# A small matmul folded into its neighbour's weights, and six scheduling edits, in a decoder block on eight cores

## The chip, the cores and the metric

One Trainium2 chip, all eight NeuronCores (two dies of four), each core working on two of the sixteen sequences. The metric is device time in microseconds (us) of the slowest core. Most executions agree within 0.3%. In some executions the cores of one die, or of both, run at a lower granted TensorE clock and the time is several per cent longer; these are called slow and are never compared with fast ones.

Every experiment ran beside the kernel before on the same chip, but not all experiments on the same chip. On the chip of the first profiles die 0 lost time to spells at 0.81 of the clock. On the chips of the later experiments these spells were nearly absent from the fast runs, so the kernel before took some 2572 us there instead of 2593.

## The reference

```python
x = x + 0.5 * swiglu(rmsnorm(x, ffn1_norm), ...)          # 1024 -> 2816 -> 1024
h = rmsnorm(x, mix_norm) @ w_in                            # pool values | q | k | v | forget logits
# pooling mixer on 512 columns: 4 groups of 128 channels, windows 2, 4, 8, 16
pooled = causal_window_mean(groups[g], w_g) - groups[g]    # along the tokens
mixed  = einsum("bsgc,gcd->bsgd", pooled, pool_w)          # along the channels
y_pool = rmsnorm(mixed * pool_scale, out_norm_pool)
y_attn = rmsnorm(forgetting_attention(q, k, v, f, ...), out_norm_attn)
x = x + concat([y_pool, y_attn]) @ w_out
x = x + 0.5 * swiglu(rmsnorm(x, ffn2_norm), ...)
```

Sixteen sequences of 2048 tokens, width 1024, 8 attention heads of 64.

## The kernel before

The two FFNs run as eight units of 1024 tokens each; the mixer (projection, pooling, attention, output projection) runs as eight tiles of 512 tokens, interleaved with the FFN units. Nobody wrote the interleaving by hand: each piece is a Python generator that yields operations, and a list scheduler picks, when the program is built, the operation that its estimates say can start first. After that the order on each engine is fixed.

```python
def emit(self, op):                                   # the scheduler's clock, cut
    ...
    done = t + cost + LAT[op.eng]
    late += cost + LAT[op.eng] + LATE                 # LATE = 300.0: pessimism, steers the order
```

Eight PSUM banks come from one pool, `MB`. Attention holds five of them through a tile. "Credits" limit how many results of one kind may be on their way:

```python
def project():                                        # cut
    for t in range(NT):
        cred = Pool_(2)                               # two results in flight: v, q, k, pool alike
        ...
        sc.spawn(pool_post(t, pb, cred), P_POST)
        for it in range(6):                           # q, q, k, k, pool, pool
            for c2 in range(2):
                yield cred
                b = yield MB
                yield Op("pe", ..., mm8(w, c2 * 1024, b, hm), ...)      # L759

def pool_post(t, banks, cred):                        # cut
    if t:
        yield ev_an[t - 1]                            # attention norm of the tile before
    for g in range(4):
        yield Op("act", ..., e.copy(out=pv[:, 16:528], in_=ps[bank][:]))      # L849
        MB.put(bank); cred.put(0)
        ... window sums on VectorE (L866) ...
        yield Op("dve", ..., scalar_tensor_tensor(out=pl, ...))               # L877: mean - input
        mb = yield MB
        yield Op("pe", ..., e.matmul(ps[mb][:], lhsT=poolw[g], rhs=pl))       # L889
        yield Op("act", ..., e.activation(out=slot(g), in_=ps[mb][:], func=Copy,
                                          scale=pool_scale))                  # L893
        MB.put(mb)

def norm_ffn(u):                                      # cut; statistics for each unit's two tiles
    for t2 in range(2):
        yield XS                                      # the one buffer for a tile of the residual
        yield from x_loads(xf, s, tt, ...)            # reload it from memory
        r, rs_ = yield from (stats_pool() if u else stats_pe(x_))   # squares summed on POOL, or on TensorE
```

Of the other lines named below: L710 is the gate/up matmul of an FFN, L736 the down matmul, L637 and L640 the ScalarE copy and the VectorE multiply that free a gate/up pair's banks, L953 and L961 attention's matmuls, L998 the ScalarE step between them, L553 the ones-matmul that sums squares, L1081 the add of the residual behind the output projection. L885 belongs to the same VectorE chain as L877.

## Time and profile before

| | before |
|---|---|
| time, median of the first 4 runs | 2589.9 us |
| TensorE busy, idle (core 1, complete trace) | 2470.4 us, 113.2 us |
| busiest other engine | ScalarE, 59% |
| idle in front of the pool_w matmul, 0.3% of the matmuls | 31.7 us |

TensorE is the bound, so the question to the profile is what its idle time consists of; the prediction below shows these lines.

### The profile page before, as it was taken

Reading aid. Unit: us, or ns where it says so; the run is one execution under the profiler, and the core shown is the slowest. Engines: PE = TensorE matmul, PEld = TensorE weight load, DVE = VectorE, ACT = ScalarE, POOL = GpSimd, SP = SyncE. Lnnn points to the kernel's source line nnn. Section 1 sums busy time; section 2 is a strip of 40 time slices with the busy share of each in tenths; the row PEclk is TensorE's granted clock in tenths of the full one; section 3 lists DMA queues with packets and bytes.
Section 4 is the critical chain, followed back from the end, with each engine's and each line's share of the span. In section 5 each row is a group of like instructions: output and inputs, shape, how many; then the busy total and the mean of one; then the engine's idle time right before and its main releaser. Section 6 shows DMA issues by size and latency. Waiting matters only on the chain.

```text
span 2588.8 us, 39912 instructions; the slowest of 8 cores (2559.3 to 2588.8 us)
## 1 busy us (share of the span) xinstructions
PE 2452.7 (95%) x11667; PEld 1063.9 (41%) x11900; DVE 1388.9 (54%) x1827; ACT 1528.5 (59%) x3137; POOL 1067.4 (41%) x1147
## 2 busy tenths in 40 slices
PE   7999998989998999999999989998999899999999
PEld 2444443434343444334444433443344344444444
DVE  2112147765667775764755847635767566642111
ACT  5562467661766835788455668257784579904650
POOL 2444435541544532545334426444354134514430
PEclk8989999999999999999999999999999999999999
DMA  7888866358635455652555242652525531275225
GB/s 169 175 210 203 225 148 170 98 161 237 174 113 158 122 180 166 174 155 66 178 172 167 103 147 75 190 171 79 180 80 172 194 109 66 66 213 162 74 66 161
DMA packets 123876, 383.56 MB, mean 148 GB/s; under 512 B 15152, under 2 KB 15280, under 8 KB 123056
## 3 DMA queue, kind: packets, MB, share of 16 engines
q0 software_dynamic: 51664, 206.33, 30.7%
q1 hardware_dynamic: 72000, 174.67, 20.3%
q8 instruction: 100, 1.64, 0.3%
q14 instruction: 112, 0.92, 0.1%
HBM read 348.05 MB, written 91.24 MB: 170 GB/s over the span
## 4 chain that ended last, share of the span: by engine, by line
PE 78%; DMA 6%; DVE 5%; issue 5%; ACT 4%; POOL 1%; SPq 0%; DVEq 0%; ACTq 0%; POOLq 0%
PE ps L710 41%; PE ps L736 20%; PE ps L759 9%; PE ps L961 2%; PE ps L953 2%; PE ps L1141 2%; DMA yT<-sb_xr 1%; DMA sb_xsF<-yT 1%; ACT sb_PT L998 1%; DMA sb_xr<-xT 1%; DVE sb_xm L866 1%; DVE sb_rs L1072 1%; PE ps L553 1%; DMA sb_wA<-wgu 1%; DMA sb_act<-xT 1%
## 5 line engine op out<-in xcount | busy, mean ns | idle before, releaser
L710 PE MATMUL ps<-sb_hF,sb_wA 128*128 128x512 bf16 x5490 | 1288.6, 388 | 34.8 <-DVE sb_sg L640 7.2
L710 PEld LDWEIGHTS ps<-sb_hF,sb_wA 128*128 128x128 bf16 x5632 | 548.9, 99 | 737.2 <-issue 189.7
L648 POOL TENSOR_TENSOR sb_act<-sb_sg 128x512 bf16<-128x512 f32 x352 | 486.6, 1383 | 464.2 <-ACT sb_sg L646 274.2
L736 PE MATMUL ps<-sb_act,sb_wB 128*128 128x512 bf16 x2752 | 631.0, 382 | 10.2 <-DVE sb_rs L1072 2.4
L998 ACT ACTIVATE sb_PT<-ps,sb_BT 128x256 bf16<-128x256 f32 (+1 forms) x1152 | 471.5, 480 | 264.1 <-PE ps L961 167.6
L640 DVE TENSOR_TENSOR sb_sg<-sb_sg,ps 128x512 f32<-128x512 f32 x352 | 239.2, 680 | 533.1 <-PE ps L710 334.5
L1026 DVE TENSOR_TENSOR sb_acc<-sb_acc,sb_PT 128x1024 f32<-128x1024 f32 (+3 forms) x288 | 381.4, 1324 | 116.8 <-ACT sb_PT L998 62.7
L736 PEld LDWEIGHTS ps<-sb_act,sb_wB 128*128 128x128 bf16 x2816 | 272.1, 98 | 347.7 <-issue 38.8
L633 ACT ACTIVATE sb_sg<-ps 128x512 f32<-128x512 f32 x352 | 214.0, 608 | 291.4 <-PE ps L710 288.0
L643 ACT ACTIVATE sb_sg<-sb_sg,sb_one_t 128x512 f32<-128x512 f32 x352 | 263.3, 748 | 0.0
L646 ACT ACTIVATE sb_sg<-sb_sg 128x512 f32<-128x512 f32 x352 | 226.8, 644 | 19.2 <-ACT sb_sg L643 0.4
L680 DVE SCALAR_TENSOR_TENSOR sb_xr<-ps,sb_xr 128x512 f32<-128x512 f32 x128 | 87.3, 684 | 232.2 <-PE ps L736 175.9
L637 ACT COPY sb_sg<-ps 128x512 f32<-128x512 f32 x352 | 209.9, 596 | 0.0
L759 PE MATMUL ps<-sb_hm,sb_wM 128*128 128x512 bf16 x755 | 179.1, 381 | 3.9 <-ACT sb_xm L893 3.2
L576 POOL TENSOR_TENSOR sb_na<-sb_na,sb_sq 128x512 f32<-128x512 f32 x132 | 167.2, 1267 | 16.5 <-ACT sb_sq L547 9.0
L547 ACT ACTIVATE sb_sq<-sb_xsF 128x512 bf16<-128x512 f32 x184 | 115.3, 653 | 77.9 <-DMA sb_xsF<-yT 51.5
L517 ACT ACTIVATE sb_rs<-ps,sb_eps_t 128x512 f32<-128x512 f32 x104 | 71.8, 694 | 111.8 <-PE ps L553 102.2
L1072 DVE RECIPROCAL sb_rs<-ps 128x128 f32<-128x128 f32 x128 | 119.2, 941 | 13.8 <-PE ps L1058 13.4
L759 PE MATMUL ps<-sb_yc,sb_wM 128*128 128x512 bf16 x503 | 117.6, 383 | 9.4 <-DVE sb_xsF L1081 8.4
L424 POOL DMA_DIRECT2D sb_wB<-wd2s x64 | 35.4, 553 | 191.0 <-PE ps L736 171.1
L759 PEld LDWEIGHTS ps<-sb_hm,sb_wM 128*128 128x128 bf16 x768 | 74.7, 98 | 95.0 <-issue 11.1
L1006 POOL TENSOR_SCALAR_AFFINE_SELECT sb_PT<-sb_PT 128x256 bf16<-128x256 bf16 x128 | 71.8, 567 | 65.4 <-ACT sb_PT L998 64.2
(87 smaller groups left out, 1632.7 us busy)
## 6 DMA issues: line engine op xcount, KB each, us to landing
sb_xsF<-yT SPq DMA_DIRECT2D x96, 512.0 KB, 6.8
sb_wA<-wgu2s POOLq DMA_DIRECT2D x88, 512.0 KB, 3.7
sb_wA<-wgu1s POOLq DMA_DIRECT2D x66, 512.0 KB, 4.4
yT<-sb_xr SPq DMA_DIRECT2D x128, 256.0 KB, 4.1
sb_wB<-wd2s POOLq DMA_DIRECT2D x64, 352.0 KB, 4.4
sb_wM<-wins POOLq DMA_DIRECT2D x42, 512.0 KB, 3.7
sb_wB<-wd1s POOLq DMA_DIRECT2D x48, 352.0 KB, 4.6
sb_xr<-xT SPq DMA_DIRECT2D x64, 256.0 KB, 4.7
```

The costliest lines, as they stand in the source:

```text
L576: lambda e, a_=a_, sl=sl: e.tensor_tensor(out=na[:], in0=a_, in1=sq_t[:, tok(sl)], op=ALU.add), c_pool(TT))
L633: lambda e: e.activation(out=sg, in_=ps[bg][:], func=AF.Exp, scale=-1.0), c_act(TT))
L637: lambda e: e.copy(out=gu, in_=ps[bg][:]), c_act(TT))
L640: lambda e: e.tensor_tensor(out=gu, in0=gu, in1=ps[bu][:], op=ALU.mult), c_dve(TT))
L643: lambda e: e.activation(out=sg, in_=sg, func=AF.Ln, bias=one_t[:, 0:1], scale=1.0), c_act(TT, False, True))
L646: lambda e: e.activation(out=sg, in_=sg, func=AF.Exp, scale=-1.0), c_act(TT, False))
L648: lambda e: e.tensor_tensor(out=act_ap(fl, t2), in0=sg, in1=gu, op=ALU.mult),
L710: ins = e.matmul(ps[b][:], lhsT=w[:, part * 1024 + kc * 128: part * 1024 + (kc + 1) * 128], rhs=hF[:, kc * 1024 + t2 * TT: kc * 1024 + (t2 ...
L736: ins = e.matmul(ps[b][:], lhsT=w[:, k:k + 128], rhs=act_ap(fl, t2), start=(fl == 0), stop=(fl == NFF - 1))
L759: ins = e.matmul(ps[bank][:], lhsT=w[:, off + kc * 128: off + (kc + 1) * 128], rhs=src[:, tok(kc)], start=(kc == 0), stop=(kc == NKC - 1))
L998: lambda e, s_=s_, a=a, z=z, hq=hq, b=b, pt=pt, c=c, j=j: e.activation(out=PT[:, pt * 1024 + s_ * TT + a: pt * 1024 + s_ * TT + z], in_=ps ...
L1026: lambda e, w=w, a_=a_: e.tensor_tensor(out=a_, in0=a_, in1=w, op=ALU.add),
```

## The change

Intent: take the pool_w matmul and its ScalarE eviction out of every tile, and smooth the schedule around the mixer.

1. **Fold.** pool_w is multiplied into the pool columns of w_in once, during the first FFN unit; pool_scale moves into the ScalarE copy of the projection.
2. **Pool credit.** The pool projection gets one credit of its own.
3. **Output credit.** The output projection gets one credit instead of two.
4. **Last unit.** The last unit's statistics move from POOL to TensorE, and its second tile is not reloaded, because it is still in the buffer.
5. **Estimates.** The scheduler's pessimism becomes 200 for TensorE, 600 for POOL.
6. A fourth buffer for the FFN's residual. 7. The second FFN's weights are converted a little later.

```diff
-LATE, LATE_DMA = 300.0, 4000.0
+LATE = {"pe": 200.0, "act": 300.0, "dve": 300.0, "pool": 600.0}
+LATE_DMA = 4000.0
@@ fold(), new, cut
+            for g in range(4):
+                for half in range(2):
+                    def mm(e, b=b, g=g, half=half):
+                        for k in range(4):
+                            ins = e.matmul(ps[b][:, k * 128:(k + 1) * 128], lhsT=hm[:, a:a + 128],
+                                           rhs=poolw[:, g * 128:(g + 1) * 128], start=True, stop=True)
+                    ... copy to PT, and PT to the folded weights in memory ...
@@ norm_ffn
-                    yield from x_loads(xf, s, tt, yT if f else xT, f)
+                    if (u, t2) != (7, 1): yield from x_loads(xf, s, tt, yT if f else xT, f)
-                r, rs_ = yield from (stats_pool() if u else stats_pe(x_))
+                r, rs_ = yield from (stats_pool() if 0 < u < 7 else stats_pe(x_, False))
@@ pool_post
-                         lambda e: e.copy(out=pv[:, 16:528], in_=ps[bank][:]), c_act(TT))
+                         lambda e: e.activation(out=pv[:, 16:528], in_=ps[bank][:], func=AF.Copy,
+                                                scale=pvec[:, 24 + g: 25 + g]), c_act(TT, True, True))
-                mb = yield MB
-                yield Op("pe", [plk, "poolw"], [("ps", mb)], ... matmul ...)
-                yield Op("act", [("ps", mb), "pvec"], [("xm", g)], ... scaled copy ...)
-                MB.put(mb)
@@ project
-                sc.spawn(pool_post(t, pb, cred), P_POST)
+                credp = Pool_(1)
+                sc.spawn(pool_post(t, pb, credp), P_POST)
-                        yield cred
+                        yield cred if it < 4 else credp
@@ outproj
-                cred = Pool_(2)
+                cred = Pool_(1)
@@ elsewhere: RR = Pool_(3) -> Pool_(4), conversion jobs at steps 6 + 7*i//4 instead of 2*i, buffers rearranged
```

More of the change, by code (lines that the diff above doesn't have):

```diff
@@ L245, in emit @@
             done = t + cost + LAT[op.eng]
-            late += cost + LAT[op.eng] + LATE
+            late += cost + LAT[op.eng] + LATE[op.eng]
         for r in op.reads:
@@ L287, in build_nc @@
     wd = [din("wd1", [NKC, 128, NFF * 128]), din("wd2", [NKC, 128, NFF * 128])]
-    win = din("win", [6, 128, 2048])
+    win = din("win", [4, 128, 2048])
+    winp_d = din("winp", [128, 4096])
     winv_d = din("winv", [2, 128, 2080])
@@ L318, in build_nc @@
         xsF = sb("xsF", [128, NKC * TT], F32)
-        xm = sb("xm", [128, NKC * 528], F32)
-        xr = sb("xr", [128, 3 * TT], F32)
+        xm = sb("xm", [128, 4 * TT + 4 * 528], F32)
+        xr = sb("xr", [128, 4 * TT], F32)
         kn = sb("kn", [128, 4 * S], BF16)
@@ L340, in build_nc @@
         bfb = sb("bfb", [128, 32], F32)
-        poolw = sb("poolw", [128, 512], BF16)
         ones_bf = sb("ones_bf", [128, 128], BF16)
@@ L345, in build_nc @@
         ones_f = sb("ones_f", [128, 128], F32)
-        gq8 = sb("gq8", [128, 1], F32)
-        eps_t = sb("eps_t", [128, 1], F32)
-        one_t = sb("one_t", [128, 1], F32)
+        cst = sb("cst", [128, 3], F32)
+        gq8, eps_t, one_t = cst[:, 0:1], cst[:, 1:2], cst[:, 2:3]
         ps = [es.enter_context(nc.psum_tensor(f"ps{b}", [128, 512], F32)) for b in range(8)]
@@ L357, in build_nc @@
         for k in range(4):
+            tr.add_dma_sem(f"wp{k}")
+            tr.add_dma_sem(f"ws{k + 4}")
             tr.add_dma_sem(f"xR{k}")
@@ L362, in build_nc @@
         tr.dma("sp", "c2", [], ["bfb"], lambda e: e.dma_start(out=bfb[:], in_=bfb_d))
-        tr.dma("pool", "cp", [], ["poolw"], lambda e: e.dma_start(out=poolw[:], in_=poolw_d))
         tr.op("dve", [], ["ones_bf"], lambda e: e.memset(ones_bf[:], 1.0))
-        tr.op("dve", [], ["eps"], lambda e: e.memset(eps_t[:], EPS))
-        tr.op("dve", [], ["one"], lambda e: e.memset(one_t[:], 1.0))
+        tr.op("dve", [], ["eps"], lambda e: e.memset(eps_t, EPS))
+        tr.op("dve", [], ["one"], lambda e: e.memset(one_t, 1.0))
         tr.op("dve", [], ["ones_f"], lambda e: e.memset(ones_f[:], 1.0))
@@ L378, in build_nc @@
         tr.op("dve", ["pvec"], ["gq8"], lambda e: e.tensor_scalar(
-            out=gq8[:], in0=pvec[:, 32:33], scalar1=0.125, scalar2=None, op0=ALU.mult))
+            out=gq8, in0=pvec[:, 32:33], scalar1=0.125, scalar2=None, op0=ALU.mult))
         MB = Pool_(8)
         FC = Pool_(6)
-        SQ, RS, SG, RR, PTP = Pool_(4), Pool_(3), Pool_(5), Pool_(3), Pool_(4)
+        SQ, RS, SG, RR, PTP = Pool_(4), Pool_(3), Pool_(5), Pool_(4), Pool_(4)
         XS = Pool_(1)
@@ L470, in items_m @@
                     for i in range(6):
-                        yield (win_s if t else win)[i], ("win", i), (None if t else win_s[i])
+                        first = t == 0 and i < 4
+                        yield (win if first else win_s)[i], ("win", i), win_s[i] if first else None
                 if t:
@@ L478, in build_nc @@
         ev_cv.update({("wd", 1, i): Ev() for i in range(2 * NKC)})
+        ev_cv.update({("win", i): Ev() for i in (4, 5)})
         ev_step = {(u, fl): Ev() for u in range(8) for fl in range(NFF)}
         def converts():
-            jobs = [(1 + 2 * i // NFF, 2 * i % NFF, wgu[1][i], wgu_s[1][i], [("wgu", 1, i)])
+            jobs = [(1 + (6 + 7 * i // 4) // NFF, (6 + 7 * i // 4) % NFF, wgu[1][i], wgu_s[1][i], [("wgu", 1, i)])
                     for i in range(NFF)]
@@ L495, in build_nc @@
         ev_act = {(u, fl, t2): Ev() for u in range(8) for fl in range(NFF) for t2 in range(2)}
-        ev_first = Ev()
+        ev_first, ev_second = Ev(), Ev()
+        LAST = NFF - NKC
         ringA = Ring("rA", wA, 3, 2048, list(items_a()),
@@ L517, in rms @@
                      lambda e: e.activation(out=rs_, in_=ps[bank][:], func=AF.Ln,
-                                            scale=1.0 / n, bias=eps_t[:, 0:1]), c_act(TT))
+                                            scale=1.0 / n, bias=eps_t), c_act(TT))
             yield Op("act", [("rs", r)], [("rs", r)],
@@ L532, in build_nc, with x_loads @@
         xf = Tile(xsF, [[("xF", kc)] for kc in range(NKC)], "xF")
-        LAST = NFF - NKC
         xa = Tile(act[:, LAST * 1024:].bitcast(F32),
                   [[("act", LAST + kc, t2) for t2 in range(2)] for kc in range(NKC)], "xA")
-        def x_loads(x_, s, tt, src, keyed):
+        def x_loads(x_, s, tt, src, keyed, after=[]):
             for kc in range(0, NKC, 2):
-                yield Op("sp", [("y", s, tt, kc + i) for i in range(2)] if keyed else [],
+                yield Op("sp", [("y", s, tt, kc + i) for i in range(2)] if keyed else after,
                          x_.keys[kc] + x_.keys[kc + 1],
@@ L555, in ones_mm, with stats_pe @@
             SQ.put(sl)
-        def stats_pe(x_):
+        def stats_pe(x_, warmup):
             bank = yield MB
@@ L563, in stats_pe @@
                 yield from ones_mm(bank, sl, kc == 0, kc == NKC - 1)
+                if warmup:
+                    yield from warm(8 if kc < NKC - 1 else 40)
                 sl = nx
@@ L593, in stats_pool, with setup, warm, mm @@
             return r, rs_
+        def setup():
+            yield Op("sp", [], ["pvec"], lambda e: e.dma_start(out=pvec[:], in_=pvec_d), 100.0, sem="c0")
+            yield Op("sp", [], ["bfb"], lambda e: e.dma_start(out=bfb[:], in_=bfb_d), 100.0, sem="c2")
+            yield Op("dve", ["pvec"], ["gq8"], lambda e: e.tensor_scalar(
+                out=gq8, in0=pvec[:, 32:33], scalar1=0.125, scalar2=None, op0=ALU.mult), 90.0)
+        def warm(n):
+            b = yield MB
+            def mm(e):
+                for _ in range(n):
+                    ins = e.matmul(ps[b][:, 0:128], lhsT=ones_bf[:], rhs=ones_bf[:], start=True, stop=True)
+                return ins
+            yield Op("pe", ["ones_bf"], [("ps", b)], mm, c_pe(n, 128))
+            MB.put(b)
@@ new lines, in fold @@
+        def fold():
+            key = ("act", 2, 0)
+            yield ev_act[(0, 2, 0)]
+            poolw = qn[:, 0:512]
+            yield Op("pool", [key], [("qn", 0)], lambda e: e.dma_start(out=poolw, in_=poolw_d),
+                     c_dma(128 * 2048), sem="cp")
+            for g in range(4):
+                yield ev_act[(0, 2 + 2 * g, 0)]
+                yield Op("pool", [("act", 2 + 2 * g, 0)], [("hm", 2 * g), ("hm", 2 * g + 1)],
+                         lambda e, g=g: e.dma_start(out=hm[:, g * 1024:(g + 1) * 1024],
+                                                    in_=winp_d[:, g * 1024:(g + 1) * 1024]),
+                         c_dma(128 * 4096), sem=f"wp{g}")
+            yield ev_act[(0, 12, 0)]
+            for g in range(4):
+                for half in range(2):
+                    b = yield MB
+                    def mm(e, b=b, g=g, half=half):
+                        for k in range(4):
+                            a = g * 1024 + (half * 4 + k) * 128
+                            ins = e.matmul(ps[b][:, k * 128:(k + 1) * 128], lhsT=hm[:, a:a + 128],
+                                           rhs=poolw[:, g * 128:(g + 1) * 128], start=True, stop=True)
+                        return ins
+                    yield Op("pe", [("qn", 0), ("hm", 2 * g + half)], [("ps", b)], mm, c_pe(4, 128))
+                    yield Op("act", [("ps", b)], [("PT", g)],
+                             lambda e, b=b, g=g, half=half: e.copy(
+                                 out=PT[:, g * 1024 + half * 512: g * 1024 + (half + 1) * 512],
+                                 in_=ps[b][:]), c_act(TT))
+                    MB.put(b)
+                if g % 2:
+                    i = 4 + g // 2
+                    yield Op("sp", [("PT", g - 1), ("PT", g)], [("win", i)],
+                             lambda e, g=g, i=i: e.dma_start(out=win_s[i],
+                                                             in_=PT[:, (g - 1) * 1024:(g + 1) * 1024]),
+                             c_dma(128 * 4096), sem=f"ws{i}")
+                    ev_cv[("win", i)].hit()
@@ L642, in pair_post @@
             yield Op("act", [("sg", sl), "one"], [("sg", sl)],
-                     lambda e: e.activation(out=sg, in_=sg, func=AF.Ln, bias=one_t[:, 0:1],
+                     lambda e: e.activation(out=sg, in_=sg, func=AF.Ln, bias=one_t,
                                             scale=1.0), c_act(TT, False, True))
@@ L750, in slot @@
         def slot(i):
-            return xm[:, i * 528: i * 528 + TT]
+            return xm[:, i * TT:(i + 1) * TT]
         def wide(i):
-            return xm[:, i * 528:(i + 1) * 528]
+            return xm[:, 4 * TT + (i - 4) * 528: 4 * TT + (i - 3) * 528]
         def mm8(w, off, bank, src):
@@ L806, in f_chain @@
                      lambda e: e.activation(out=fz[:, 32:64], in_=fz[:, 32:64], func=AF.Ln,
-                                            bias=one_t[:, 0:1], scale=1.0), c_act(32))
+                                            bias=one_t, scale=1.0), c_act(32))
             b = yield MB
@@ L847, in pool_post @@
                 pv, pk = wide(pi), ("xm", pi)
-                yield Op("act", [("ps", bank)], [pk],
-                         lambda e: e.copy(out=pv[:, 16:528], in_=ps[bank][:]), c_act(TT))
+                yield Op("act", [("ps", bank), "pvec"], [pk],
+                         lambda e: e.activation(out=pv[:, 16:528], in_=ps[bank][:], func=AF.Copy,
+                                                scale=pvec[:, 24 + g: 25 + g]), c_act(TT, True, True))
                 MB.put(bank)
@@ L872, in pool_post @@
                     ti = 13 - ti
-                pt = yield SQ
-                pl = sq_t[:, tok(pt)]
-                plk = ("sq", pt)
+                pl, plk = slot(g), ("xm", g)
                 yield Op("dve", [sk, pk], [plk],
@@ L886, in pool_post @@
                                                        in1=pv[:, 16:16 + w - 1], op=ALU.subtract), 90.0)
-                mb = yield MB
-                yield Op("pe", [plk, "poolw"], [("ps", mb)],
-                         lambda e: e.matmul(ps[mb][:], lhsT=poolw[:, g * 128:(g + 1) * 128], rhs=pl,
-                                            start=True, stop=True), c_pe(1, TT))
-                SQ.put(pt)
-                yield Op("act", [("ps", mb), "pvec"], [("xm", g)],
-                         lambda e: e.activation(out=slot(g), in_=ps[mb][:], func=AF.Copy,
-                                                scale=pvec[:, 24 + g: 25 + g]), c_act(TT, True, True))
-                MB.put(mb)
             for g in range(4):
@@ L1158, in project @@
                         if it < 2:
-                            sc.spawn(qk_post(b, qn[:, tok(c)], ("qn", c), gq8[:, 0:1], "gq8", ev_qkf[t],
+                            sc.spawn(qk_post(b, qn[:, tok(c)], ("qn", c), gq8, "gq8", ev_qkf[t],
                                              cred), P_POST)
@@ L1251, in build_nc @@
         sc.spawn(converts(), P_LOAD)
+        sc.spawn(fold(), P_LOAD)
         sc.run()
@@ L1268, in _prep_weights @@
     wi = w_in[:, 0:1536].reshape(8, 128, 12, 128).transpose(2, 1, 0, 3)
-    order = [4, 5, 6, 7, 8, 9, 10, 11, 0, 1, 2, 3]
-    wi = wi[order].reshape(6, 2, 128, 8, 128).transpose(0, 2, 1, 3, 4).reshape(6, 128, 2048)
+    wi = wi[4:].reshape(4, 2, 128, 8, 128).transpose(0, 2, 1, 3, 4).reshape(4, 128, 2048)
+    winp = w_in[:, 0:512].reshape(8, 128, 4, 128).transpose(3, 2, 0, 1).reshape(128, 4096)
     wv = w_in[:, 1536:2048].reshape(8, 128, 2, 256)
@@ L1290, in _prep_weights @@
         "wd1": lay_d(inp["ffn1_w_down"]), "wd2": lay_d(inp["ffn2_w_down"]),
-        "win": f(wi), "winv": f(winv), "wout": f(wo), "poolw": f(poolw),
+        "win": f(wi), "winp": f(winp), "winv": f(winv), "wout": f(wo), "poolw": f(poolw),
         "pvec": pvec, "bfb": f(bfb),
```

## The prediction

> **What bounds the kernel now.** I read the cores first, then engine busy shares and slices, then the waits of TensorE, then its idle time by stage, then one window in order of time.
>
> The page's head and slices (tenths busy; PEclk is the granted TensorE clock):
>
> ```profile
> span 2588.8 us, 39912 instructions; the slowest of 8 cores (2559.3 to 2588.8 us)
> PE 2452.7 (95%) x11667; PEld 1063.9 (41%) x11900; DVE 1388.9 (54%) x1827; ACT 1528.5 (59%) x3137; POOL 1067.4 (41%) x1147
> PE   7999998989998999999999989998999899999999
> PEclk8989999999999999999999999999999999999999
> ```
>
> TensorE is the bound: 95% busy, with 2588.8 - 2452.7 = 136 us idle on core 0. The real figure is nearer 115, since core 0's trace lacks some 230 records that the others have, and core 1 shows 2470.4 us busy in 2583.6. Nothing else passes 59%. So a gain must come from less matmul work, from fewer idle us of TensorE, or from its clock.
>
> Who TensorE waited for (us in total, times, longest), the largest first, two others left in for scale:
>
> ```profile
> PE ps L889 <- DVE sb_sq L877: 18.5, 7, 4.7
> PE ps L553 <- ACT sb_sq L547: 17.2, 3, 12.6
> PE ps L759 <- DVE sb_xsF L1081: 8.4, 9, 1.7
> PE ps L710 <- DVE sb_sg L640: 7.2, 13, 0.8
> ...
> PE ps L710 <- ACT sb_xm L893: 4.8, 6, 0.9
> PE ps L710 <- ACT sb_xm L849: 4.6, 1, 4.6
> ...
> PE ps L759 <- ACT sb_xm L893: 3.2, 6, 0.9
> ```
>
> L889 is the little pool_w matmul of the pooling mixer, L877 the VectorE instruction that makes its input, L893 the ScalarE copy that empties its bank, L849 the copy of the pool projection. L553/L547 (17.2) is the program's start and stays. The group of L889, with its idle time before, and who ended it:
>
> ```profile
> L889 PE MATMUL ps<-sb_sq,sb_poolw 128*128 128x512 bf16 x31 | 12.2, 395 | 31.7 <-DVE sb_sq L877 18.5 <-ACT sb_sg L637 4.1 <-DVE sb_sg L640 3.0
> ```
>
> 31 recorded matmuls, 0.3% of all, own 31.7 us of idle time: a quarter of all that there is. The stage where it happens, 750 to 800 us (TensorE, its loads, VectorE, ScalarE, POOL busy us; clock; DMA share), and inside it:
>
> ```profile
> 750.00:800.00 50.00, 39.62 (x179) 15.84 (x181) 35.55 (x39) 38.67 (x81) 25.48 (x23) 0.97 0.32 88
> ```
>
> ```profile
> 781.08 0.69 DVE L877 SCALAR_TENSOR_TENSOR sb_sq<-sb_xm 128x512 bf16<-128x512 f32 x1 [0.17 <-DVE sb_xm L866]
> 781.69 0.68 DVE L640 TENSOR_TENSOR sb_sg<-sb_sg,ps 128x512 f32<-128x512 f32 x1
> 782.03 0.59 PE L889 MATMUL ps<-sb_sq,sb_poolw 128*128 128x512 bf16 x1 [4.21 <-DVE sb_sq L877]
> 782.51 1.27 POOL L648 TENSOR_TENSOR sb_act<-sb_sg 128x512 bf16<-128x512 f32 x1 [2.17 <-DVE sb_sg L640]
> 782.52 9.11 PE L710 MATMUL ps<-sb_hF,sb_wA 128*128 128x512 bf16 x35
> ```
>
> The pool_w matmul stood at the head of TensorE's queue 4.21 us before VectorE finished its window sums; 35 gate/up matmuls then ran without a break. The instruction order is fixed when the program is built, by a list scheduler's estimates, so an estimate that is too early becomes a stall. Each of the eight tiles has such a dip (400, 500, 750, 1000, 1500, 1750, 2000 us: 39 to 46 of 50 us busy).
>
> **What the Trainium skill says.** (1) "TensorE: Matmul & The Clock Gate", "Step-by-step: what each phase is for": matmuls stay in program order, only weight loads move ahead. The lines above agree. (2) Same page, "Wait — 56ns, not 53.3ns?": warm start to start about 215.7 ns at 512 columns, 55.6 at 128. The chain shows 49 matmuls in 10.74 us, with 0.38 us for the last: (10.74 - 0.38)/48 = 216 ns, so the 388 ns mean durations overlap. (3) Same page, "Seeing it yourself": with three or more cores of a die on dense matmul, a limiter takes the die to 13/16 of its clock. The trace shows only a mean of 0.92 in the first 350 us, but 0.98 to 1.00 in most stretches later. (4) "ScalarE: Activation LUTs", "What ACT_TABLE_LOAD costs": a pointer operand adds about 93 ns. Here 585 ns (L849, plain) against 692 (L893, pointer scale): 107.
>
> **The change, part by part.**
>
> *Fold of pool_w.* Window mean minus input acts along tokens, pool_w along channels, so they commute: pool_w is multiplied into the pool columns of w_in once, pool_scale goes into the projection's copy.
> - Removed from TensorE: 32 matmuls x 0.216 = 6.9 us.
> - Removed idle: of L889's 31.7 us, 18.5 + 1.4 (L877, L885) waited for the pooling chain itself. I count 80%, 15.9, since the next instruction was ready in the window shown. The other 11.8 waited for ScalarE or VectorE to free a bank (L637, L640, L998 and others); the next gate/up pair wants a bank from the same place, so I count 40%, 4.7.
> - Removed idle behind L893: 4.8 + 3.2 + 0.9 = 8.9 us on banks held by its result. 70%, 6.2.
> - ScalarE: 32 x 0.692 = 22.1 us go, the projection's copy gains 32 x 0.107 = 3.4, and 8 set-up copies of 0.59 add 4.7. Net -14 us, off the path.
> - Added: 32 matmuls of 128 columns x 0.056 = 1.8 us in the first FFN unit, and I put 2 us on their waiting for weights or banks. Their loads (four of 128x1024 float32, 2 MB) replace two 1 MB loads of the first tile's projection but come earlier, where the DMA share is 0.81 to 0.93 and TensorE already lost 3.4 us on a weight load: 3 us more.
> - Sum: 6.9 + 15.9 + 4.7 + 6.2 - 1.8 - 2 - 3 = 26.9 us.
>
> *Credits.* Pool projection on its own single credit: at most one bank, not two, waits for the previous tile's attention norm. The 4.6 us on L849 is that wait; half, 2.3. Output projection 2 to 1 credits: its 8.4 us on L1081 is TensorE waiting for a bank behind VectorE; one in flight lets FFN work between. Half, 4.2.
>
> *Last unit.* Its norm statistics go from POOL back to TensorE (two tiles: 16 ones-matmuls for 4, +12 x 0.216 = 2.6 us) and the second tile's reload is skipped, the residual still being in place. POOL loses some 2 x 10.8 us. The rows from 2350 us on show 49.74 of 50 us busy, with no gap before the last unit: the saved latency was hidden. Cost 2.6.
>
> *Scheduler estimates* (matmul lateness 300 to 200, POOL 300 to 600), a fourth residual slot, later weight conversion: only order and depth. Waits for POOL (4.4 at L553, 2.4 at L961) and for the residual (1.3) may shrink; I give 2.5, and treat reordering as noise of some 8 us either way. Conversion leaves the first six steps of the second unit, where TensorE is 99% busy anyway: 0.
>
> Total: 26.9 + 2.3 + 4.2 - 2.6 + 2.5 = 33.3 us, so 2589.9 - 33.3 = 2556.6. I take 2556.
>
> **The rivals.** (a) *The wait only moves.* VectorE still does the window sums (about 18 us per tile in one stream), and gate/up banks are freed by L640 in that stream, while attention holds five of eight banks. Then TensorE stalls a little later at L710 <- L640 or L637. For: 11.8 of the 31.7 us were bank waits, and L640 already shows 7.2 in 13 short stalls. Against: 1050 to 1300 us runs 99% busy with the same banks held. It would leave some 12 us: 2578. (b) *The full gain.* All 31.7 + 8.9 + 4.6 + 8.4 us idle and 6.9 of work go, less 9 of costs: 2538, still just about 2%. It needs every wait to vanish. For: VectorE and ScalarE are under 80% busy in the dips. Against: a build-time order is never that exact. (c) *The clock takes it back.*[...] For: the first 350 us lose 8% so, and die 0 at 0.978 is 22 us slower than die 1 at 0.989. Against: at 1050 to 1300 us the clock is 1.00 with TensorE 99% busy, and the dips lie where it is 0.93 to 1.00. It would cost up to 10 us. (d) *The first unit becomes DMA-bound* by the fold's loads: up to 10 us lost, 2566.
>
> **Range and chances.** The middle is 33 us. Rivals (a) and (d) pull it to 12 to 24, (b) to 52, the reordering moves any by 8. Eight times in ten: 2539 to 2576. Faster by over 2% means below 2538, beyond the full gain of (b): 0.11. Slower by over 2% would need a new stall of 52 us: 0.01. Within 2%: 0.88.
>
> **What would show it.** The idle time of TensorE falls from 136 to about 105 (by core 0's incomplete count); no line waits for L877 any more; the 50 us rows of the dips rise from about 40 to 45 or more. Rival (a): L710 <- L640 and <- L637 grow from 9.5 us to over 25. Rival (c): the same or less idle, but the mean clock under 0.97. Rival (d): L710 <- DMA of weights over 8 us within the first 250. The ones-matmuls of the last unit should show no wait of over 2 us. I am wrong if the rows before 350 us or after 2350 us move by more than 10 us, or if the dips keep their depth with another name on the wait.

## More of the kernel before

One more view matters afterwards, which the prediction did not ask for: narrower stretches around the dip at 780 us (columns: stretch, its length, busy us and instruction count of TensorE, its weight loads, VectorE, ScalarE and POOL, then the granted TensorE clock, the DMA share and GB/s).

```profile
779.00:782.00 3.00, 0.00 (x0) 0.01 (x1) 2.83 (x4) 0.48 (x1) 1.33 (x2) 0.92 0.56 153
782.00:786.00 4.00, 3.92 (x11) 1.46 (x13) 2.29 (x4) 1.86 (x4) 3.35 (x4) 0.63 0.05 16
786.00:790.00 4.00, 4.00 (x21) 1.81 (x19) 2.81 (x5) 4.00 (x10) 0.98 (x2) 1.00 0.78 131
```

First TensorE stands still for 3 us. In the next 4 us it is "busy" 98% of the time but at a mean clock of 0.63, and completes 11 matmuls; in the 4 us after that, at full clock, 21. An idle stretch is followed by a slow one, and the slow one counts as busy.

## The result

The changed kernel took 2542.0 us (median of 10 runs, 2530.6 to 2887.9) against 2592.6 (median of 16). The ratio is 0.9805, 95% interval 0.9787 to 0.9824, about 50 us less. A ratio here and below is the mean time of one kernel's fast runs over that of the other's of the same rounds, so it is not quite the ratio of the medians. The time is inside the predicted range, nearer its fast end; faster by 2% or not is unclear at this margin.

The page of the changed kernel, its head and the slices of TensorE:

```profile
span 2535.5 us, 40100 instructions; the slowest of 8 cores (2506.4 to 2535.5 us)
PE 2452.5 (97%) x11912; PEld 1061.6 (42%) x11912; DVE 1393.8 (55%) x1827; ACT 1510.3 (60%) x3113; POOL 1034.7 (41%) x1133
...
PE   7999998999999999999999999999999999999999
```

The slowest core is now core 1. Its idle time is 2535.5 - 2452.5 = 83 us against 113.2 for the same core before: 30 of its 48 us. The other 18 are busy time, though the change removes only 2.5 us of matmul work by the prediction's count. Up to 8 of the 18 lie in the spells at 0.81 of the clock, 147 us on this core and 189 before, so this pair of profiles is not quite even. What TensorE waited for now (us in total, times, longest; L770 is the gate/up matmul, L700 and L697 free its banks, L556 is the ones-matmul, L819 the mixer's projections, L914 a VectorE instruction of the pooling chain):

```profile
PE ps L770 <- DVE sb_sg L700: 12.8, 8, 2.7
PE ps L556 <- DVE sb_sg L700: 9.0, 5, 2.2
PE ps L819 <- DMA sb_wM<-wins: 8.5, 3, 4.5
PE ps L770 <- DVE sb_xm L914: 4.8, 2, 2.8
PE ps L770 <- ACT sb_sg L697: 4.3, 7, 1.6
```

The waits on the pool_w matmul, on its eviction and on the output projection's residual add (8.4 us, now 1.2) are gone or nearly so. Gate/up pairs wait longer for their banks (L770 on L700 and L697: 17.1 us, on the slowest core before 9.5), and there is a new wait of 8.5 us for the mixer's weights. It comes with the fold: 6.8 us in "fold only" below, none in "all but the fold". The dip shown before, the same 50 us:

```profile
750.00:800.00 50.00, 47.81 (x218) 19.53 (x217) 32.78 (x43) 43.54 (x89) 29.53 (x28) 0.94 0.44 107
```

47.8 us busy instead of 39.6, still with a spell at a lower clock.

**Where the time went, summed up.** Busy is the time with a matmul running, idle is the span less that. The trace also records the spells of half clock (0.50), which I added up; inside them matmuls start 427 ns apart, elsewhere 216 (medians). Means over the cores whose trace is complete (for half clock over all). The second pair comes from later runs on chips with hardly any spells at 0.81, so it is the cleaner one.

| profile | span | TensorE idle | TensorE busy | at half clock |
|---|---|---|---|---|
| before, first | 2571.8 | 119.8 | 2452.0 | 52.1 |
| after, first | 2522.2 | 82.9 | 2439.3 | 34.2 |
| before, again | 2564.4 | 125.9 | 2438.4 | 49.2 |
| after, again | 2516.0 | 89.8 | 2426.2 | 32.7 |

Clean pair: 48.4 us = 36.1 of idle time + 12.2 of busy time. Not all time at half clock is busy: on the cores with a complete trace TensorE ran matmuls in 35.2 us of it before and 25.5 after. At half clock a matmul takes twice as long, so these 9.7 us less are some 4.9 us of the 12.2. The work removed is 2.5 more; the rest, some 5 us, stays open. The prediction had 31 and 2.5.

### The profile page after: what moved, and what is told of

Read it like the earlier page. It is cut to its first block, busy times and chain, and to the rows that moved or that the text cites. A ratio compares the mean times of both kernels' runs of the same rounds, so it can differ in the third digit from the quotient of the medians.

```text
span 2535.5 us, 40100 instructions; the slowest of 8 cores (2506.4 to 2535.5 us)
## 1 busy us (share of the span) xinstructions
PE 2452.5 (97%) x11912; PEld 1061.6 (42%) x11912; DVE 1393.8 (55%) x1827; ACT 1510.3 (60%) x3113; POOL 1034.7 (41%) x1133
## 4 chain that ended last, share of the span: by engine, by line
PE 82%; DMA 6%; DVE 4%; ACT 3%; issue 3%; SPq 0%; POOL 0%; DVEq 0%; ACTq 0%; POOLq 0%
PE ps L770 40%; PE ps L796 22%; PE ps L819 10%; PE ps L1011 3%; PE ps L1003 3%; DMA yT<-sb_xr 2%; PE ps L1191 2%; DMA sb_wM<-wins 1%; DMA sb_xsF<-yT 1%; PE ps L556 1%; ACT sb_PT L1048 1%; DVE sb_xm L927 1%; DMA sb_act<-xT 1%; DVE sb_acc L1076 1%; ACT sb_sq L550 1%
## 5 line engine op out<-in xcount | busy, mean ns | idle before, releaser
L770 PE MATMUL ps<-sb_hF,sb_wA 128*128 128x512 bf16 x5632 | 1298.5, 385 | 30.0 <-DVE sb_sg L700 12.8
L770 PEld LDWEIGHTS ps<-sb_hF,sb_wA 128*128 128x128 bf16 x5632 | 545.1, 99 | 729.0 <-issue 153.3
L708 POOL TENSOR_TENSOR sb_act<-sb_sg 128x512 bf16<-128x512 f32 x352 | 474.7, 1349 | 466.3 <-ACT sb_sg L706 266.6
L700 DVE TENSOR_TENSOR sb_sg<-sb_sg,ps 128x512 f32<-128x512 f32 x352 | 239.5, 681 | 513.7 <-PE ps L770 211.4
L703 ACT ACTIVATE sb_sg<-sb_sg,sb_cst 128x512 f32<-128x512 f32 x352 | 261.9, 744 | 0.0
L697 ACT COPY sb_sg<-ps 128x512 f32<-128x512 f32 x352 | 209.6, 595 | 2.5 <-POOL sb_act L708 2.5
L819 PE MATMUL ps<-sb_hm,sb_wM 128*128 128x512 bf16 x768 | 183.6, 386 | 8.9 <-DMA sb_wM<-wins 8.5
L581 POOL TENSOR_TENSOR sb_na<-sb_na,sb_sq 128x512 f32<-128x512 f32 x120 | 154.0, 1283 | 11.4 <-ACT sb_sq L550 7.0
L521 ACT ACTIVATE sb_rs<-ps,sb_cst 128x512 f32<-128x512 f32 x104 | 70.9, 687 | 110.8 <-PE ps L556 110.6
L819 PE MATMUL ps<-sb_yc,sb_wM 128*128 128x512 bf16 x512 | 122.0, 381 | 1.2 <-DVE sb_xsF L1131 1.2
L819 PEld LDWEIGHTS ps<-sb_hm,sb_wM 128*128 128x128 bf16 x768 | 75.8, 99 | 102.8 <-issue 16.5
L1056 POOL TENSOR_SCALAR_AFFINE_SELECT sb_PT<-sb_PT 128x256 bf16<-128x256 bf16 x128 | 66.3, 524 | 82.7 <-ACT sb_PT L1048 81.9
```

The costliest lines, as they stand in the source:

```text
L581: lambda e, a_=a_, sl=sl: e.tensor_tensor(out=na[:], in0=a_, in1=sq_t[:, tok(sl)], op=ALU.add), c_pool(TT))
L697: lambda e: e.copy(out=gu, in_=ps[bg][:]), c_act(TT))
L700: lambda e: e.tensor_tensor(out=gu, in0=gu, in1=ps[bu][:], op=ALU.mult), c_dve(TT))
L703: lambda e: e.activation(out=sg, in_=sg, func=AF.Ln, bias=one_t, scale=1.0), c_act(TT, False, True))
L708: lambda e: e.tensor_tensor(out=act_ap(fl, t2), in0=sg, in1=gu, op=ALU.mult),
L770: ins = e.matmul(ps[b][:], lhsT=w[:, part * 1024 + kc * 128: part * 1024 + (kc + 1) * 128], rhs=hF[:, kc * 1024 + t2 * TT: kc * 1024 + (t2 ...
```

## The experiments

Twelve runs, each beside the kernel before. All gave correct results. "us" is the gain: one less the ratio, times 2572. The last three columns, in us of one profiled execution, are as in the table above (for "before + pool credit" of its undisturbed die alone).

| run | ratio (95%) | us | idle | busy | half clock |
|---|---|---|---|---|---|
| before, again | 0.9995 (0.9974 to 1.0015) | 1 | 125.9 | 2438.4 | 49.2 |
| after, again | 0.9821 (0.9805 to 0.9838) | 46 | 89.8 | 2426.2 | 32.7 |
| fold only | 0.9928 (0.9896 to 0.9960) | 19 | 110.2 | 2436.0 | 66.3 |
| all but the fold | 0.9859 (0.9837 to 0.9882) | 36 | 91.5 | 2433.9 | 34.9 |
| before + pool credit | see text | 22 | 103.6 | 2436.5 | 54.1 |
| before + two pool credits | 1.0002 (0.9963 to 1.0041) | 0 | 125.9 | 2439.9 | 48.1 |
| before + output credit | 1.0057 (1.0044 to 1.0070) | -15 | 134.4 | 2443.1 | 56.6 |
| before + estimates | 1.0032 (1.0020 to 1.0045) | -8 | 129.2 | 2438.7 | 57.0 |
| after, pool credit undone | 0.9893 (0.9839 to 0.9946) | 28 | 99.1 | 2433.5 | 51.3 |
| after, last unit undone | 0.9854 (0.9802 to 0.9906) | 38 | 100.0 | 2427.6 | 50.8 |
| after, output credit undone | 0.9812 (0.9768 to 0.9855) | 48 | 91.7 | 2430.0 | 39.9 |
| after, estimates undone | 0.9826 (0.9802 to 0.9850) | 45 | 91.2 | 2426.6 | 31.5 |

### before again

No edit.

> The kernel before against itself, to see the scatter and the granted clocks of many fast runs. All theories: ratio 1.000 within 0.002. If the higher clock that the changed kernel's profile showed (die 0 at 0.983 against 0.978, die 1 at 0.993 against 0.989) was chance, the fast runs here reach 0.983 and 0.993 in about half of the cases; if the changed kernel brings it about, they stay near 0.978 and 0.989.

Measured: ratio 0.9995. The mean clock of its fast runs, over all cores, is 0.990, as for the other runs of the kernel before on that chip (0.990), while "all but the fold" and "after, estimates undone" have 0.993 and 0.994 on the same chip. The test as it was set, with 0.983 and 0.993, cannot be read on a chip that has hardly any spells at 0.81; but the two relatives of the changed kernel show that the higher clock is not chance. It belongs to the kernel.

### fold only

The changed kernel with items 2 to 7 undone:

```diff
-LATE = {"pe": 200.0, "act": 300.0, "dve": 300.0, "pool": 600.0}
+LATE = {"pe": 300.0, "act": 300.0, "dve": 300.0, "pool": 300.0}
-                credp = Pool_(1)
+                credp = cred
-                cred = Pool_(1)          # output projection
+                cred = Pool_(2)
# residual buffers, conversion steps, last unit: as before
```

> The fold of pool_w alone; scheduler estimates, credits, residual slots, conversion times and last unit as before. Theory A (the prediction's sum): the fold carries most, 27 us of gain, ratio 0.9895. Theory B (the surplus over the prediction comes from the fold, as the pooling waits vanish whole): 40 us or more, ratio 0.985 or less. Theory C (the scheduler's estimates carry the surplus): 27 us or less, ratio 0.9895 or more.

Measured: 0.9928, 19 us. Theory B is out, and A's 27 us lies just outside the interval (10 to 27 us). C's number fits; its cause, the estimates, is tested below and is out. Where the rest went, in the waits of TensorE in this run (L677 is the VectorE instruction that writes an FFN's normalised input):

```profile
PE ps L770 <- DVE sb_sg L700: 24.3, 11, 4.8
...
PE ps L770 <- DVE sb_hF L677: 6.1, 3, 4.5
```

The pool_w matmul is gone and with it 34.8 us of idle time in front of it (on the kernel before's page of the same job), but gate/up pairs now wait 24.3 us for L700 to free a bank; before it was 6.9. Idle time fell by 15.7 us only, and the time at half clock even rose, from 49 to 66 us. Part of the wait moved, as the prediction's first rival said.

But that is not where most of the gain was lost. The last FFN unit has the same 1056 gate/up and down matmuls in every kernel here, so a run can be cut at its first gate/up matmul (means of the cores with a complete trace). Up to there "fold only" is 33 us ahead of the kernel before: 2298.0 us against 2330.8, with 25.8 us less idle time. From there to the end it takes 248.3 us against 233.6. This kernel still has the old last unit, with its statistics on POOL (L589), and core 5 shows the wait, from 2240 to 2340 us, then the busy row:

```profile
PE ps L770 <- DVE sb_hF L677: 5.3, 2, 4.5
PE ps L556 <- POOL sb_sq L589: 4.2, 1, 4.2
```

```profile
2240.00:2340.00 100.00, 89.53 (x397) 39.13 (x395) 26.03 (x39) 34.67 (x60) 32.76 (x36) 0.93 0.52 166
```

So the fold alone gains more than was predicted, and pays half of it back in the last unit.

### all but the fold

The kernel before with items 2 to 5 and 7. The fourth residual buffer does not fit beside the pool_w tile.

```diff
+LATE = {"pe": 200.0, "act": 300.0, "dve": 300.0, "pool": 600.0}
+                credp = Pool_(1)         # pool projection
+                cred = Pool_(1)          # output projection
# last unit and conversion steps: as changed
```

> Everything but the fold: new lateness estimates, single credits, conversion times, last unit; three residual slots, since the fourth does not fit beside the pool_w tile. Theory A: 6 us of gain, ratio 0.9975. Theory B: 0 to 6 us, ratio 0.9975 to 1.000. Theory C: 15 to 25 us, ratio 0.990 to 0.994, with the waits on the pool_w matmul's chain (18.5 us before) cut by at least half though the matmul is still there.

Measured: 0.9859, 36 us, more than any theory named. The matmul is still there in all eight tiles (the lines have moved down by one):

```profile
L890 PE MATMUL ps<-sb_sq,sb_poolw 128*128 128x512 bf16 x32 | 12.3, 384 | 19.2 <-DVE sb_sq L878 11.2 <-DVE sb_sg L641 4.8 <-DVE sb_sq L886 3.2
```

Its idle time fell from 34.8 to 19.2 us without its removal; the waits on its own chain fell by 40%, not by the half that Theory C asked for. Put the fold and the fourth residual buffer on top and one has the changed kernel: idle time 91.5 to 89.8, busy time 2433.9 to 2426.2. Once the other edits are in, the fold is worth about the matmul work that it removes, some 7 us, and next to no waiting.

### after, estimates undone

```diff
-LATE = {"pe": 200.0, "act": 300.0, "dve": 300.0, "pool": 600.0}
+LATE = {"pe": 300.0, "act": 300.0, "dve": 300.0, "pool": 300.0}
```

> The changed kernel with the old lateness estimate of 300 for every engine. Theories A and B: within 5 us of the changed kernel, ratio to before 0.979 to 0.982. Theory C: at least 12 us slower than the changed kernel, ratio 0.985 or more.

Measured: 0.9826, within the scatter of the changed kernel (0.9821 and 0.9805). Theory C's 0.985 is at the very end of the interval; with "before + estimates" below it is out.

### before + pool credit

```diff
-                sc.spawn(pool_post(t, pb, cred), P_POST)
+                credp = Pool_(1)
+                sc.spawn(pool_post(t, pb, credp), P_POST)
-                        yield cred
+                        yield cred if it < 4 else credp
```

> The kernel before with one edit: the pool projection gets a single credit of its own instead of sharing the two credits of the value, query and key projections. The run without the fold gained 36 us, of which the prediction explains 6, so one of four small edits must carry it. Theory D (banks: two results of the pool projection that wait for the previous tile's attention norm hold two of the three banks that attention leaves): most of it comes from here, 15 us or more, ratio 0.994 or less, and the waits on L849 and L893 (4.6 and 8.9 us before) go. Theory E (order: the new lateness estimates): 5 us or less, ratio 0.998 or more.

Measured: no ratio, since seven of its eight runs had a slow die. The one fast run took 2552.9 us, against 2567.9 to 2574.4 for eight fast runs of the kernel before. The dies that the slow runs left undisturbed say the same. In its profile die 1 is undisturbed; die 1 in the fast run "before again", on another chip, stands second:

```profile
die 1 (median of its cores): 2543.3 us, clock 0.990
```

```profile
die 1 (median of its cores): 2562.5 us, clock 0.990
```

The mean span of the undisturbed dies in its seven slow runs is 2539 us; of all cores in the fast runs of the kernel before on its own chip, 2562. So some 22 us from one line. In front of the pool_w matmul, on core 7 of the undisturbed die and then on the kernel before:

```profile
L889 PE MATMUL ps<-sb_sq,sb_poolw 128*128 128x512 bf16 x32 | 12.8, 400 | 20.5 <-DVE sb_sq L877 11.5 <-DVE sb_sg L640 4.7 <-DVE sb_sq L885 3.5
```

```profile
L889 PE MATMUL ps<-sb_sq,sb_poolw 128*128 128x512 bf16 x32 | 12.7, 398 | 34.8 <-DVE sb_sq L877 16.8 <-DVE sb_sq L885 7.3 <-ACT sb_sg L637 5.0
```

14 of the 22 us show up here, at the matmul that the fold removes: in part, fold and credit remove the same waiting. Theory D holds: no wait on L849 shows, and those on L893 are 1.1 us against 9.7. This kernel, too, pays in its old last unit: on die 1 it reaches it at 2296.4 us, some 33 us early, and then takes 243.7 us where the kernel before takes 233.6.

### before + two pool credits

As above, with `credp = Pool_(2)`.

> The kernel before with the pool projection on two credits of its own. It tells apart why one own credit gained 20 us. If it is that fewer results of the pool projection hold banks: no gain or a loss, ratio 0.999 or more. If it is that the pool projection no longer shares with the queries and keys: as much gain as with one, ratio 0.990 to 0.994.

Measured: 1.0002. Not sharing with q and k is worth nothing; allowing only one pool result at a time is worth 22 us. That agrees with banks being what is short (attention holds five of eight, two waiting pool results leave one). No view counts banks, but the traces allow it: a pool result holds its bank from the first of its eight matmuls to the end of its ScalarE copy. Summed over the 32 results, us per core (cores with a complete trace; of die 1 alone for "before + pool credit"), and the time in which two or more held a bank at once:

| run | banks held | two or more at once |
|---|---|---|
| before, again | 398 | 126 |
| before + two pool credits | 433 | 139 |
| before + pool credit | 202 | 1 |
| fold only | 135 | 23 |
| after, pool credit undone | 140 | 25 |
| after, again | 104 | 0 |

One credit ends the double holding, two credits do not. The fold ends most of it too, which fits the overlap of the two edits. A rival remains in principle: any edit reshuffles the fixed order, and other small edits moved the time by up to 15 us. Against it, the credit gains in two different kernels, and the double holding ends with it both times.

### before + output credit

```diff
-                cred = Pool_(2)          # output projection
+                cred = Pool_(1)
```

> The kernel before with one edit: one credit instead of two in the output projection. Prediction: the wait on the residual add (8.4 us before) at least halves, 4 us of gain, ratio 0.998. Theory D2 (this credit carries the unexplained 30 us): 15 us or more, ratio 0.994 or less. If it is neither, 0.997 to 1.000.

Measured: 1.0057, 15 us slower, which no theory had. The waits of gate/up for the pool_w matmul's eviction (L893) grew from 5.6 to 12.8 us:

```profile
L710 PE MATMUL ps<-sb_hF,sb_wA 128*128 128x512 bf16 x5632 | 1284.8, 383 | 42.4 <-ACT sb_xm L893 12.8 <-DVE sb_sg L640 10.3 <-ACT sb_sg L633 6.2
```

28.7 us of idle time before gate/up in the kernel before, 42.4 here, while the wait that the edit aims at (L759 on L1081) fell only from 8.4 to 6.6 us. I read it as a reshuffled order that met the mixer at a worse moment; the run does not prove that.

### before + estimates

The first two lines of the diff alone.

> The kernel before with one edit: lateness estimates of 200 for TensorE and 600 for POOL instead of 300 for all. Theory E (the fixed order of instructions was the fault, so the estimates carry the unexplained gain): 15 us or more, ratio 0.994 or less, and the waits of the pool_w matmul on its chain fall from 18.5 us to 11 or less. Theory D: within 5 us, ratio 0.998 to 1.002; the changed kernel with the old estimates was only some 5 us slower.

Measured: 1.0032, 8 us slower. Theory E is out: the matmul's wait on its chain is still 14.3 us, not 11 or less. D's "within 5 us" was missed as well.

### after again

No edit.

> The changed kernel unaltered, on the same chip as the single edits. All theories: ratio 0.979 to 0.982. The two-speed reading (part of the gain is time that TensorE spends at half clock after long idle stretches, 50 us per core before and 34 after in the first traces): again 30 to 38 us at half clock per core; the reading that the clock was chance: as much as in the kernel before, 46 to 55.

Measured: 0.9821, and 32.7 us at half clock per core, inside the stated 30 to 38. The smaller time at half clock repeats.

### after, last unit undone

```diff
-                    if (u, t2) != (7, 1): yield from x_loads(xf, s, tt, yT if f else xT, f)
+                    yield from x_loads(xf, s, tt, yT if f else xT, f)
-                r, rs_ = yield from (stats_pool() if 0 < u < 7 else stats_pe(x_, False))
+                r, rs_ = yield from (stats_pool() if u else stats_pe(x_, False))
```

> The changed kernel with the last unit as before: statistics on POOL, second tile reloaded. The prediction called this part a cost of 2.6 us, so undoing it should gain: ratio 0.978 to 0.981 (the changed kernel: 0.982 on this kind of chip). Theory F (the latency that the kernel before hides comes into the open once the other parts have moved the last unit ahead; two kernels with the old last unit showed 6 us of stalls there and TensorE at 0.93 of its clock): 8 to 15 us slower than the changed kernel, ratio 0.985 to 0.988, with waits for L677 or for the POOL statistics of 5 us or more at the start of the last unit.

Measured: 0.9854, 8 us slower than the changed kernel by the ratios. The intervals overlap, but the fast runs do not: 2532.8 to 2542.8 against 2521.8 to 2530.9 on the same chip. In the trace it is plain. Waits of TensorE in this run from 2220 to 2330 us, where the last unit begins, and the busy row of that stretch:

```profile
PE ps L556 <- POOL sb_sq L589: 5.6, 1, 5.6
PE ps L770 <- DVE sb_hF L677: 5.3, 2, 4.5
```

```profile
2220.00:2330.00 110.00, 98.26 (x450) 42.64 (x448) 37.80 (x51) 24.59 (x45) 32.90 (x41) 0.94 0.57 180
```

and the same stretch of the changed kernel ("after again"), where TensorE waited for nothing:

```profile
2220.00:2330.00 110.00, 110.00 (x521) 49.30 (x519) 39.59 (x54) 35.15 (x65) 28.91 (x37) 1.00 0.54 172
```

11.7 us idle, and a mean clock of 0.94 on top: 450 matmul records against 521. From the first gate/up matmul of the unit to the end this run takes 249.1 us, the changed kernel 233.5. Theory F holds. The kernel before, which has the same code here, has no gap at its own start of the last unit (80.00 of 80 us busy from 2290 to 2370 us on core 5 of "before again").

### after, pool credit undone

```diff
-                credp = Pool_(1)
+                credp = cred
```

> The changed kernel with the pool projection on the shared two credits again. Alone in the kernel before, its own single credit was worth some 20 us. If that adds up with the fold: 15 us or more lost, ratio 0.988 or more. If the fold and the single credit removed much the same waits: within 6 us of the changed kernel, ratio 0.980 to 0.984.

Measured: 0.9893, 18 us slower than the changed kernel by the ratios, whose intervals just fail to meet; its fast runs took 2540.8 to 2553.6 us, the changed kernel's 2521.8 to 2530.9. The wait for gate/up banks is the largest of the run, above the program's start:

```profile
PE ps L770 <- DVE sb_sg L700: 30.0, 17, 5.0
```

In the changed kernel it is 12.8 to 14.3 us. So the credit also carries what the fold alone could not: without it, part of the fold's freed time turns into bank waits. By the test as it was set, 18 us is the side of "adds up" (15 or more). The traces say half: up to the last unit the credit is worth 16.6 us here (2299.1 against 2282.5), some 33 in the kernel before.

### after, output credit undone

As "before + output credit", the other way.

> The changed kernel with two credits in the output projection again. Alone in the kernel before, one credit cost 15 us. If that holds here, this kernel beats both: ratio 0.977 or less. If the prediction's reading holds (the credit spares 4 us of waits on the residual add): 4 us slower, ratio 0.984. If small edits only reshuffle the fixed order: anywhere within 8 us of the changed kernel.

Measured: 0.9812 against 0.9821, which fits the third reading, a mere reshuffle.

## Why the prediction was right or wrong

The predicted mean was 2556 us with a range of 2539 to 2576; the time was 2542. Right range, and the sum was 15 us short. Its parts were further off than the sum, in opposite directions, so that the sum came so near is in part luck. Of the signs that it named, most came true: no line waits for L877, the wait for gate/up banks stayed under 25 us (17.1), the mean clock over 0.97. Its list of dips, said to be one for each of eight tiles, has seven.

- **"TensorE is the bound", gain from its idle time: right.** Idle time fell by 36 us of 126, the prediction said 31.
- **Fold, 26.9 us: about right up to the last unit, and then spoilt there.** Alone it gave 19 us in all. Up to the last unit it gave 33, with 25.8 us less idle time where the prediction's terms come to 21.8 (15.9 + 4.7 + 6.2 removed, 2 + 3 added). The 15 us lost after that belong to the step "the saved latency was hidden" below. The shares of 80%, 40% and 70% were not tested one by one; the 80% rest on one window in which 35 matmuls followed at once, and the wait for L700, which rose to 24.3 us, shows that elsewhere the next instruction was not ready. The 6.9 us of matmul work were right (7.7 us of busy time between "all but the fold" and "after, again", with the half-clock share in it). So was the set-up: the 32 small matmuls start 56 ns apart, 1.8 us in all. What was missed of its cost is the 8.5 us wait for the mixer's weights. Rival (d), a first unit bound by loads, did not show: 1.6 us of waits for weights in the first unit's ring on core 1, 4.9 on core 0 of the repeat, where 8 was the sign.
- **Pool credit, 2.3 us: the mis-sized term.** It is worth some 18 to 22 us. The step took the one line that named L849 (4.6 us) as the cost of two banks held up, but two banks were held at once for 126 us per core. A bank shortage is not named after the one who holds the bank: it showed as waits for L877, L885, L637 and L893 in front of other instructions.
- **Output credit, 4.2 us: not there.** 15 us worse alone, nothing in the changed kernel; why it was worse stays open.
- **Last unit, a cost of 2.6 us: wrong in sign.** It is worth 8 us by the ratios, 13 by the fast runs on one chip. The step that failed: no gap in the old profile, so "the saved latency was hidden". It was hidden by the very idle time that the other parts removed. They bring TensorE to the last unit some 50 us earlier (2278.5 us in "after, last unit undone", 2330.8 before), and then the POOL statistics and the reload stand in its way: 15.6 us.
- **Estimates and the rest, 2.5 us, order as noise of 8 us:** the estimates alone cost 8 us and give nothing in the end. The noise of order was set too small: one edit of a credit moved the time by 15 us.
- **Rival (c), the clock takes gain back: wrong in sign, and missing from the sum.** Spells at 0.81 are one thing; the spells at half clock, which follow idle stretches, are another. With fewer idle stretches they shrank from 49 to 33 us per core, some 5 us of gain.
- **Rivals.** (a), the wait only moves, describes a part of the fold alone; (b), the full gain at 2538, is nearest to the result of all, but by other parts than it names.

The parts do not add up: fold alone 19, all the rest 36, together 46. Up to the last unit they are 33, 39 and 48 us: fold and pool credit free in part the same banks, and the fold alone also pays in the last unit. The later conversion and the fourth residual buffer were not tried by themselves, so their share stays open, as does the reason for the new wait of 8.5 us for the mixer's weights.

## What to carry to other kernels

A wait in front of an instruction tells where the engine stood, not what was short. Where many stages share a pool of banks, limit how many results of one stage may hold one, before deleting work. A latency that is hidden in the profile before is hidden only as long as the engine in front of it is late, so price it again at the new speed. And an idle stretch of TensorE of 2 us or more can cost 1.7 us on top, half of a 3.4 us spell at half clock behind it: of 239 such stretches after the first 30 us, on the 24 cores with a complete trace of the two kernels and their repeats, 162 had a spell begin in them or within 3.5 us after, of 1870 shorter ones 84 (those that began inside a spell left out).

## What the Trainium skill lacked or had wrong

- "TensorE: Matmul & The Clock Gate", "HAM oscillation — how this bites in real kernels", gives the rule as no TensorE gaps over some 3.4 us. Here shorter ones were enough. On the 24 cores with a complete trace (the two kernels and their repeats) I looked at the 6.8 us ahead of each of the 199 spells at half clock, those at the program's end left out. Each had at least 1.8 us of idle time there, but for 134 no single gap that touches this stretch was over 3.4 us. On core 7 of the kernel before at 1508 us, 2.9 us of idle time in gaps of 1.0 us at most led to a spell. The page's next section tells of a kernel in which short idles do this, but gives no length for them. That each spell is 3.4 us long, or a multiple, agrees with the page's window.
- "Perfetto Trace Analysis", "Identifying Performance Opportunities", says that consistent bubbles can mean that there is not enough SBUF or PSUM for the next tile. This case agrees (banks held by pool results, above), but the page does not say how to find who holds the banks: here the holder's own line stood for 4.6 us of waits, and limiting it was worth some 20.
